# Gate projections by seven half products instead of eight, with a searched instruction order

## The chip, the cores and the metric

The kernel runs on all eight NeuronCores of one Trainium2 chip (cores 0 to 3 are one die, 4 to 7 the other). Each core computes its own share of the batch; nothing is exchanged. The metric is the device time of the slowest core in microseconds (us). In some executions, of any kernel, the cores of one or both dies show a lower granted TensorE clock and the time is longer; these are called slow (one die over 1% longer than the other at a lower clock, or the time over 1.5% above the same kernel's fastest), the others fast. Only fast executions are compared here, or, where said, the cores of an undisturbed die.

The profile's names for the engines of a core: PE is TensorE (matmuls), PEld its weight loads, DVE VectorE, ACT ScalarE, POOL GpSimd and SP SyncE. POOL and SP also issue transfers, each through its own queue; 16 DMA engines carry them. PSUM is the memory that the matmuls write to.

## The reference, cut to what matters

Four layers (D = 1024, depth 4) over 2048 prompt tokens and 64 sample tokens per core. Each layer is a chain of projections around a recurrent branch and a short convolution:

```python
h = layer_norm(x) * (1 + scale) + shift
u = h @ w_in                       # eight blocks of 1024 columns each
a_x, a_z, b_cg, b_bg, b_x, b_z, g_a, g_b = split(u)
o_a = (rglru(conv4(a_x)) * silu(a_z)) @ w_a_out
o_b = (b_bg * conv3(b_cg * b_x) * silu(b_z)) @ w_b_out
merged = sigmoid(g_a) * o_a + sigmoid(g_b) * o_b       # g_a and g_b: the two gate projections
x = layer_norm(ALPHA * x + gate * (merged @ w_o)) * ln_g + ln_b
```

The gate projections are 2 of the 11 large 1024 x 1024 products of a layer.

## The kernel before: the parts that the argument touches

The work of a core is cut into 12 slots (4 layers x 3 jobs of W = 704 tokens, HW = 352 = half a job). In each slot the first part of one job (six projections, convolutions, recurrence) is interleaved with the second part of the job before it (gates, branch outputs, output projection). The kernel writes down its operations with their dependences, and a planner in it, a list scheduler with a cost for each operation, decides the order on every engine before the program is built. The order is then fixed.

A projection of 128 output columns is 16 matmuls: 8 pieces of the contraction times 2 halves of the tokens, into one of four PSUM blocks.

```python
def mm(blk, steps, reads, tiles=(0, 1), first=True, last=True):
    def fn(e):
        for i, (w, mov) in enumerate(steps):
            for t in tiles:
                ins = e.matmul(PS[blk.pair][:, P0 + t * HW:P0 + (t + 1) * HW], w, mov(t), start=first and i == 0,
                               stop=last and i == len(steps) - 1)
        return ins
...
        for j in range(NCH):                     # 8 column groups of a slot
            def f_g(o, j=j, x=x):                # a gate: 16 matmuls, then tanh out of PSUM
                n = U.get((k, "p2", j, o))
                blk = Blk()
                mm(blk, [(wcol(WB[n], kc, 1), tile(hn, kc)) for kc in range(NCH)], [WBB[n]] + hnB)
                t = x["t" + o] = Tmp()
                act(T(t), ps(blk), AF.Tanh, [blk], [t], scale=0.5, psum=True)
            def f_o(o, j=j, x=x):                # a branch output: 16 matmuls, then gate times it
                ...
```

Weights come from HBM in fp32 and are cast to bf16 by the DMA that POOL's queue issues (`WB<-wmain`), into a ring of 8 buffers; two units for each column group.

## Time and profile before

| | before |
|---|---|
| median of 3 executions | 2721.45 us (2719.65 to 2864.68) |
| busy share of TensorE, DVE, ACT, POOL (page, slow execution) | 98%, 65%, 60%, 38% |
| matmuls per core | 18,164 |

The profile that came with the kernel fell in a slow execution of 3043 us. These are the lines of its page for the span, the busy times (engine, busy us, share, count) and the chain of work that ended last.

```profile
span 3043.2 us, 53658 instructions; the slowest of 8 cores (2984.2 to 3043.2 us)
...
PE 2972.4 (98%) x18164; PEld 1848.5 (61%) x18164; DVE 1965.9 (65%) x2316; ACT 1825.6 (60%) x2456; POOL 1158.3 (38%) x1290
...
PE 94%; DVE 2%; issue 1%; ACT 1%; DMA 1%; POOL 0%; ACTq 0%; DVEq 0%; POOLq 0%
```

TensorE is what bounds the kernel. The view of stretches of the same execution, core 0, has for each stretch the busy time and count of PE, PEld, DVE, ACT and POOL, then the granted clock, the DMA share and GB/s:

```profile
1216.00:1520.00 304.00, 303.58 (x1697) 183.40 (x1695) 199.93 (x236) 175.04 (x246) 119.21 (x143) 0.81 0.67 112
...
2432.00:2736.00 304.00, 302.62 (x2026) 198.48 (x2025) 229.41 (x259) 216.48 (x288) 132.53 (x129) 1.00 0.75 127
```

The first row runs at a clock of 0.81, the second at 1.00. At full clock a stretch of 1428 matmuls of 352 columns takes 213.5 us, 149.5 ns each. The Trainium skill, "TensorE: Matmul & The Clock Gate", Part 1, gives N/2.4 + 2.5 ns between warm matmuls, which makes an estimate of 149 ns for 352 columns, and a 13/16 limit of the clock for a die under load; both fit these numbers.

TensorE is idle for 2720.6 - 2639.4 = 81 us. By its list of waits (who waited for whom: us in total, times, longest), the largest part is the start, and nothing in the rest is large:

```profile
PE PS L971 <- DMA WB<-wc: 32.8, 7, 20.4
PE PS L479 <- ACT TMP L446: 10.3, 15, 2.7
PE PS L479 <- DVE TMP L455: 7.8, 10, 1.1
```

### The profile page before, as it was taken

The numbers are of one execution on the slowest core, as the hardware profiler recorded it, in microseconds if no ns is written. First come the engines' busy times: TensorE is split into PE (matmuls) and PEld (weight loads), VectorE is DVE, ScalarE is ACT, GpSimd is POOL, SyncE is SP. The second block draws the span as 40 slices with busy tenths as digits, with TensorE's granted clock in tenths as the row PEclk, the third lists the DMA queues.
The fourth block names the chain that finished last, engine by engine and source line by source line (L and its number), as shares of the span: only waits on it lengthen the run. The fifth ranks groups of instructions, "written<-read, shape, count | busy, mean of one in ns | idle before, by whom it ended". The sixth has DMA issues, their size and how long they took to land.

```text
span 3043.2 us, 53658 instructions; the slowest of 8 cores (2984.2 to 3043.2 us)
## 1 busy us (share of the span) xinstructions
PE 2972.4 (98%) x18164; PEld 1848.5 (61%) x18164; DVE 1965.9 (65%) x2316; ACT 1825.6 (60%) x2456; POOL 1158.3 (38%) x1290
## 2 busy tenths in 40 slices
PE   4999999999999999999999999999999999999997
PEld 2556666666666566666566666666666666666664
DVE  5666556757745664676676466458778578575674
ACT  4675547546654754655475466457667677675563
POOL 2444243334423423343442334245344345243431
PEclk8888888888888888888888888889999999999998
DMA  9669867766876786676687668777878769768774
GB/s 186 123 90 158 151 102 129 136 102 111 158 121 103 128 143 97 111 133 109 93 151 142 98 105 157 112 113 137 149 111 171 132 100 173 128 109 171 116 137 119
DMA packets 117114, 389.00 MB, mean 128 GB/s; under 512 B 13040, under 2 KB 15344, under 8 KB 116848
## 3 DMA queue, kind: packets, MB, share of 16 engines
q0 software_dynamic: 84160, 307.01, 65.3%
q1 hardware_dynamic: 32688, 78.56, 8.7%
q8 instruction: 152, 2.49, 0.3%
q14 instruction: 114, 0.93, 0.1%
HBM read 653.33 MB, written 36.27 MB: 227 GB/s over the span
## 4 chain that ended last, share of the span: by engine, by line
PE 94%; DVE 2%; issue 1%; ACT 1%; DMA 1%; POOL 0%; ACTq 0%; DVEq 0%; POOLq 0%
PE PS L479 93%; DMA WB<-wmain 1%; DVE TMP L459 1%; ACT TMP L446 1%; PE PS L971 1%; DVE TMP L455 0%; DVE LNR L455 0%; DVE TMP L697 0%; ACT L446 0%; POOL TMP L455 0%; DVE SM L455 0%; DVE X L459 0%; POOL X L485 0%; POOL WB L485 0%; DVE PS L455 0%
## 5 line engine op out<-in xcount | busy, mean ns | idle before, releaser
L479 PE MATMUL PS<-HN,WB 128*128 128x352 bf16 x12288 | 2150.3, 340 | 10.6 <-DVE TMP L455 2.7
L479 PEld LDWEIGHTS PS<-HN,WB 128*128 128x128 bf16 x12288 | 1285.1, 105 | 803.2 <-issue 15.1
L485 POOL DMA_DIRECT2D WB<-wmain x528 | 295.0, 559 | 1327.1 <-PE PS L479 1102.4
L446 ACT ACTIVATE TMP<-PS 128x704 f32<-128x704 f32 (+1 forms) x525 | 393.5, 753 | 596.0 <-PE PS L479 544.9
L446 ACT ACT_TABLE_LOAD x320 | 410.6, 1283 | 189.0 <-PE PS L479 138.5
L459 DVE SCALAR_TENSOR_TENSOR TMP<-PS,PRM,TMP 128x704 f32<-128x704 f32 (+4 forms) x467 | 430.8, 923 | 94.7 <-ACT PST L446 38.4
L455 POOL TENSOR_TENSOR TMP<-TMP 128x704 f32<-128x704 f32 (+1 forms) x225 | 392.4, 1748 | 187.9 <-ACT TMP L446 89.2
L459 DVE SCALAR_TENSOR_TENSOR TMP<-TMP,PS 128x704 f32<-128x704 f32 x192 | 170.0, 885 | 342.8 <-PE PS L479 341.4
L479 PE MATMUL PS<-MG,WB 128*128 128x352 bf16 x1536 | 273.7, 338 | 3.0 <-DVE MG L455 2.2
L479 PE MATMUL PS<-YB,WB 128*128 128x352 bf16 x1536 | 273.5, 337 | 0.0
L479 PE MATMUL PS<-YA,WB 128*128 128x352 bf16 x1536 | 273.0, 337 | 0.0
L455 DVE TENSOR_TENSOR PS<-PS,TMP 128x704 f32<-128x704 f32 x96 | 86.2, 898 | 239.4 <-ACT PS L446 133.9
L479 PEld LDWEIGHTS PS<-MG,WB 128*128 128x128 bf16 x1536 | 159.8, 105 | 101.6 <-issue 3.8
L479 PEld LDWEIGHTS PS<-YB,WB 128*128 128x128 bf16 x1536 | 159.5, 104 | 96.7
L479 PEld LDWEIGHTS PS<-YA,WB 128*128 128x128 bf16 x1536 | 159.5, 104 | 96.6
L446 ACT ACTIVATE TMP<-PS,PRM 128x704 f32<-128x704 f32 x187 | 166.3, 890 | 55.5 <-PE PS L479 38.4
L455 POOL TENSOR_TENSOR YB<-TMP 128x704 bf16<-128x704 f32 x92 | 179.1, 1947 | 53.0 <-DVE TMP L459 43.2
L446 ACT ACTIVATE TMP<-PS,HB 128x704 f32<-128x704 f32 x189 | 158.1, 845 | 66.7 <-PE PS L479 62.9
L446 ACT ACTIVATE TMP<-TMP 128x704 f32<-128x704 f32 (+1 forms) x237 | 185.1, 782 | 5.8 <-DVE MOD L459 1.4
L446 ACT ACTIVATE TMP<-X 128x704 f32<-128x704 f32 x176 | 135.0, 784 | 86.5 <-DVE X L459 66.6
L697 DVE TENSOR_TENSOR_SCAN TMP<-TMP,PST 128x704 f32<-128x704 f32 x92 | 164.4, 1787 | 30.0 <-POOL TMP L455 24.9
L455 DVE TENSOR_TENSOR TMP<-X,TMP 128x704 f32<-128x704 f32 (+1 forms) x181 | 164.8, 943 | 27.3 <-ACT TMP L446 25.1
(94 smaller groups left out, 2021.4 us busy)
## 6 DMA issues: line engine op xcount, KB each, us to landing
WB<-wmain POOLq DMA_DIRECT2D x528, 512.0 KB, 7.5
xres<-X SPq DMA_DIRECT2D x72, 352.0 KB, 12.7
X<-xres SPq DMA_DIRECT2D x72, 352.0 KB, 7.9
WB<-wc POOLq DMA_DIRECT2D x48, 512.0 KB, 7.6
X<-x SPq DMA_DIRECT2D x40, 352.0 KB, 7.7
y<-X SPq DMA_DIRECT2D x16, 352.0 KB, 13.3
X<-x POOLq DMA_DIRECT2D x8, 352.0 KB, 9.7
y<-X SPq DMA_DIRECT2D x16, 176.0 KB, 1.9
```

What stands on the lines that cost most here:

```text
L446: return P.add("act", lambda e: e.activation(out=res(out), in_=res(in_), func=func, **kw), reads, writes, cost=0.14 + 0.09 * nap + n * 0.0 ...
L455: return P.add(eng, lambda e: e.tensor_tensor(out=res(out), in0=res(in0), in1=res(in1), op=op), reads, writes, cost=cost, lat=0.05, port=n ...
L459: return P.add("dve", lambda e: e.scalar_tensor_tensor(out=res(out), in0=res(in0), scalar=scalar, in1=res(in1), op0=op0, op1=op1), reads, ...
L479: ins = e.matmul(PS[blk.pair][:, P0 + t * HW:P0 + (t + 1) * HW], w, mov(t), start=first and i == 0, stop=last and i == len(steps) - 1)
L485: return P.add(eng, lambda e: e.dma_start(out=res(out), in_=src), reads, writes, dma=tag, cost=0.56 if eng == "pool" else 0.08, nbytes=nbytes)
L697: P.add("dve", lambda e: e.tensor_tensor_scan(out=T(m)(), data0=T(r)(), data1=T(i)(), initial=PST[:, l, c, 0:1], op0=ALU.mult, op1=ALU.add ...
L971: ins = e.matmul(PS[blk.pair][:, h * 17:(h + 1) * 17], wcol(wb, kc, h), SCTb[:, kc, :], start=(kc == 0), stop=(kc == NCH - 1))
```

## The change

The intent is to take matmuls off TensorE. In 11 of the 12 slots the two gate projections of a column group are computed together by Strassen's scheme (in a form with 7 products of halves and reused sums): 7 x 4 = 28 matmuls in place of 32. For it, DVE makes four sums of the tokens per slot and four sums of the weights per column group, in bf16. The weight sums are made once per layer, stored in HBM, and read back in the other slots of the layer. Partial results hop between PSUM banks by ACT copies and DVE additions. The second part of the change is in the planner: new constants and buffer counts, and, for every group of four TensorE operations, a seed of random priorities that was found by a search (DRAWS). Core of the diff:

```diff
-NT = 18
+NT = 14
-NX = 4
-P23_FROM, P23_SPAN = 0.01, 0.85
-PE_WINDOW, EW_WINDOW = 16, 60
-QUANT = 0.25
-PE_SLACK = 1.5
+NX = 8
+P1_AT = {'ax': 0.5, 'az': 1.5, 'bz': 2.5706, 'bx': 4.207, 'gr': 4.3037, 'cg': 4.853, 'bg': 5.4886, 'gi': 6.5}
+P23_SPAN = 0.7599
+PE_WINDOW = 18
+QUANT = 0.1027
+PE_SLACK = 0.9744
  ... (more constants)
+DRAWS = (0, 0, 0, 0, 0, 0, 0, 24770, 24954, ...)      # one seed for each four TensorE operations
+            draw = DRAWS[turn] if turn < len(DRAWS) else 0
+                        if draw:
+                            key, order = key + draws[at][0], i + draws[at][1]
  ...
+    def fast_pair(k, name, hn, hnB):
+        one, two = Blk(True), Blk(True)               # two of the four PSUM blocks at once
+        c, a = one.banks
+        e, b = two.banks
+        product(a, 1, (one, two), a11, b11, [aB] + lo, True)
+        hop = act(lambda: v2(HW, W), lambda: v1(HW, W), AF.Copy, [a], [b], n=HW, psum=True)
+        product(c, 0, (), s1, t1, [bB, TSB[0]], True)
+        hop = act(T(s5, 0, HW), lambda: v1(0, HW), AF.Copy, [c], [s5], n=HW, psum=True)
+        product(b, 1, (), s2, t2, [bB, TSB[1]], False)
+        product(a, 1, (), a12, b21, [aB] + hi, False)
+        hop = tt("dve", lambda: v1(0, HW), lambda: v2(HW, W), T(s5, 0, HW), ALU.add, [b, s5], [c], n=HW, psum=True)
+        product(b, 1, (), s3, t3, [aB, TSB[2]], False)
+        hop = tt("dve", lambda: v2(0, HW), lambda: v2(HW, W), T(s5, 0, HW), ALU.add, [b, s5], [e], n=HW, psum=True)
+        product(c, 0, (), s4, b22, [bB] + hi, False)
+        product(b, 1, (), a22, t4, [aB, TSB[3]], False)
  ...
+        fast = k >= 1
+        makes = k == 1 or k > 1 and q == 0            # these slots make the weight sums and store them
+                src = (src, None) if makes else tuple(Stored(wsum_d[u, :, h * 2048:min(3584, (h + 1) * 2048)],
+                                                             wsumB[u][h], (2048, 1536)[h]) for h in range(2))
```

A gate unit read back takes two buffers of the ring of 8 (512 KB and 384 KB, on SP's queue) instead of one.

## The prediction

> What bounds it now. By the page, TensorE is busy 98% of the span; the chain of work that ended last is 94% TensorE. The profile fell in a slow execution (3043 us against a 2721 us median): the per-core list gives clocks of 0.874 to 0.895. By the stretch table core 0 ran at 0.81 up to about 2000 us and at 1.00 afterwards, core 3 the other way round. 1428 matmuls take 213.5 us at full clock (149.5 ns each), 262 take 47.3 us at 0.81 (180.6 ns). The Trainium skill, "TensorE: Matmul & The Clock Gate", Part 1, gives 352/2.4 + 2.5 = 149 ns for a warm matmul of 352 columns, and a 13/16 current limit on a die; the trace agrees with both. Joining core 3's first 1000 us (full clock) with core 0's course from the same weight load on (about 1190 us), scaled to full clock, gives about 2710 us. So the fast executions run at about full clock.
>
> At full clock 17,280 bf16 matmuls x 149.5 ns = 2583 us, the conditioning and norm matmuls about 45 us; some 85 us are start (39 us before the first large matmul, then a cold clock), tail (19 us idle in the last 83) and hardly 10 us of idle in the whole middle. No other engine is near: DVE 65%, ACT 60%, POOL 38%.
>
> What the change does. In 11 of 12 slots each of 8 column groups computes its two gate projections with 7 x 4 half matmuls instead of 32: 352 matmuls less, x 149.5 ns = 52.6 us, all on the critical engine: 1.93%.
>
> It adds, off the critical engine: 176 half-width ACT copies (352 wide out of PSUM: 0.454 us, 80 us in all), 176 half-width DVE additions on PSUM (0.52 us, 91 us), 44 token sums of 1408 bf16 and 128 weight sums of 512; scaled from the 1.02 us of a 704-wide fp32 addition these are at most 90 and 95 us, about half if bf16 goes faster. DVE so rises from 65% to at most 84%, ACT to about 70%. 56 weight loads move from POOL's queue (casting) to SP's, already in bf16; 32 units are written once. None of this should bind.
>
> The new risk is the ping-pong through PSUM: 352 times a product waits for a copy or addition of an earlier product. Counting in the built order how much TensorE work stands between (x 149.5 ns): median above 2.5 us, but 16 have 0.6 us or less and 38 under 1.0 us, against about 0.9 us for the round trip (0.45 to 0.52 us of work plus signalling). That is about 6 us of stalls if the other engines are on time, more when they are late; the tight ones gather in the last slot, where no other slot's projections fill in. The searched order can win only from start, tail and the 10 us of middle idle: I give it 5 to 12 us.
>
> 2721 - 53 + 6 - 9 = 2665 us, ratio 0.979: just at the border of 2%. Range 2648 to 2686.
>
> What would show it: 17,812 matmul records (against 18,164, give or take missing ones), still near 149.5 ns at full clock; TensorE still the chain's 90% and more; idle of TensorE before products released by ACT or DVE below 15 us in total; DVE busy up by 130 to 270 us, ACT by 80 to 110 us; start still about 39 us to the first large matmul.
>
> What would make it wrong: late hops, because ACT or DVE serves another wait first, stalling all 88 pairs by a microsecond (then 2700 or above); SP's queue holding weight loads behind stores; DVE sums slowing POOL in the scan path; the order's gain existing only in the planner; or a clock that differs between the kernels.

## More of the kernel before

Because a slow profile is a poor measure of idle time, I later ran the unchanged kernel again and got a fast profile of it (span 2720.6 us). This is what the new kernel will be compared with. Lines of its page (span, busy times, DMA queues with packets, MB and share of the engines' time, chain):

```profile
span 2720.6 us, 53658 instructions; the slowest of 8 cores (2715.0 to 2720.6 us)
...
PE 2639.4 (97%) x18164; PEld 1730.7 (64%) x18164; DVE 1974.4 (73%) x2316; ACT 1819.2 (67%) x2456; POOL 1160.6 (43%) x1290
...
q0 software_dynamic: 84160, 307.01, 69.2%
q1 hardware_dynamic: 32688, 78.56, 9.4%
...
PE 85%; DVE 6%; issue 4%; ACT 3%; DMA 2%; POOL 1%; DVEq 0%; ACTq 0%; POOLq 0%; SPq 0%
```

## The result, and the profile after

The new kernel took 2708.83 us (median of 4 fast executions, 2705.34 to 2711.49) against 2720.9 us. The ratio is 0.9955 with a 95% interval of [0.9938, 0.9973]. All ratios here are the mean time of one kernel's fast runs over that of the other's of the same rounds, so not quite the ratio of the medians. So 12 us were gained where 56 had been forecast: clear of the noise, but under 2%. The same lines of the page of its fast profile:

```profile
span 2703.8 us, 54846 instructions; the slowest of 8 cores (2676.4 to 2703.8 us)
...
PE 2594.0 (96%) x17812; PEld 1689.5 (62%) x17812; DVE 2107.1 (78%) x2664; ACT 1869.7 (69%) x2617; POOL 1120.2 (41%) x1234
...
q0 software_dynamic: 76096, 277.64, 61.8%
q1 hardware_dynamic: 58032, 159.32, 17.8%
...
PE 81%; DMA 7%; DVE 4%; issue 3%; ACT 3%; POOL 1%; DVEq 0%; ACTq 0%; SPq 0%; POOLq 0%
```

The matmuls did go: 18,164 - 17,812 = 352. TensorE's busy time fell by 2639.4 - 2594.0 = 45.4 us. But its idle time rose from 81.2 to 2703.8 - 2594.0 = 109.8 us, which gives 28.6 us back. DMA's share of the chain rose from 2% to 7%. The list of waits of the same core, core 2, shows a single wait of 12.1 us that before did not have, for stored sums, and almost nothing for the hops themselves (L597 is the line of the half products):

```profile
PE PS L1205 <- DMA WB<-wc: 33.2, 8, 20.6
PE PS L597 <- DMA WB<-wsum: 12.1, 1, 12.1
PE PS L585 <- DVE TMP L565: 10.0, 12, 2.7
PE PS L585 <- DMA WB<-wmain: 7.8, 7, 3.0
...
PE PS L597 <- DVE PS L561: 1.5, 6, 0.5
...
PE PS L597 <- ACT PS L552: 0.7, 2, 0.4
```

The view of the cores tells something else. In the new kernel, first fence, neighbouring cores end up to 26 us apart; in before (the fast profile of the repeat), second fence, 5.5 us:

```profile
core 0: 2676.4 us, clock 0.995
core 1: 2702.8 us, clock 0.992
core 2: 2703.8 us, clock 0.992
core 3: 2694.2 us, clock 0.993
```

```profile
core 0: 2715.6 us, clock 0.995
core 1: 2715.1 us, clock 0.995
core 2: 2715.0 us, clock 0.995
core 3: 2720.5 us, clock 0.993
```

Which core of a pair is the slow one changes from run to run, but in the eight fast runs of the new kernel (four here, four in a repeat below) 31 of the 32 pairs 0/1, 2/3, 4/5, 6/7 ended 9 us or more apart; in the eight fast runs of before in e1 and e17 below, none of 32 pairs did (8.9 us at most). The Trainium skill, "HBM Reference", Specifications, says that two neighbouring cores share an HBM domain and its bandwidth. The pairs agree with it; it makes memory traffic a suspect, since the new kernel writes 65.6 MB to HBM against 36.3 MB and moves 159 MB against 79 MB through the hardware queue (q1 above). In sum it is little: reads of HBM fall from 653.3 to 646.0 MB, so all of it grows by 3%. If traffic is the cause, it is more likely by when it comes than by how much there is.

The end of core 2 in the view of stretches (columns as before), and then the order of its TensorE instructions around the wait:

```profile
2605.00:2633.00 28.00, 27.56 (x183) 17.41 (x181) 17.10 (x23) 12.01 (x19) 3.17 (x6) 1.00 0.99 258
2633.00:2646.00 13.00, 0.92 (x7) 0.44 (x6) 0.89 (x1) 0.76 (x1) 0.53 (x1) 0.65 1.03 209
2646.00:2662.00 16.00, 13.65 (x73) 7.95 (x72) 5.32 (x7) 1.98 (x3) 0.00 (x0) 0.82 0.14 42
```

```profile
2633.06 0.76 PE L597 MATMUL PS<-TS,WB 128*128 128x352 bf16 x4
2645.89 2.51 PE L597 MATMUL PS<-TS,WB 128*128 128x352 bf16 x8 [12.08 <-DMA WB<-wsum]
2648.19 3.67 PE L585 MATMUL PS<-YB,WB 128*128 128x352 bf16 x16
```

For 41 us the core's DMA engines are full (share 0.99, then 1.03): in the last slot the final stores `y<-X`, the reads `X<-xres` and the stored sums all come at once. The last load of stored sums took 25.5 us from issue to landing, against a median of 5.5 us over the run; on core 0, which had come there earlier, it took 13.7 us and nobody waited. In this profile five of the eight cores have one such wait, of 11.8 to 13.4 us, and cores 0, 4 and 7 none or one of less than 6 us. It is about half of the distance between core 2 and core 0: core 2 began the same products 13 us after core 0 before it waited at all. On core 2 SP's queue waited six times, 17.5 us in all, for stores `y<-X` to land between 2600 and 2630 us, the last time just before it issued that load; on core 0, between 2586 and 2616 us, it waited for them seven times, 9.7 us. After the wait TensorE restarts at a lower clock: 16 matmuls take 3.67 us, where the same 16 take 2.55 us elsewhere in this core's trace. The skill's TensorE page, Part 1, says that an idle window of some 3.4 us halves the clock; the 0.65 and 0.82 in the clock column agree, and a narrower stretch, 2637 to 2650 us, shows 0.50 where the stretch just before (2633.9 to 2636.7) shows 1.00: the clock fell some 3 us after TensorE had gone idle.

### The profile page after: what moved, and what is told of

Read it like the earlier page. It is cut to its first block, busy times and chain, and to the rows that moved or that the text cites. A ratio compares the mean times of both kernels' runs of the same rounds, so it can differ in the third digit from the quotient of the medians.

```text
span 2703.8 us, 54846 instructions; the slowest of 8 cores (2676.4 to 2703.8 us)
## 1 busy us (share of the span) xinstructions
PE 2594.0 (96%) x17812; PEld 1689.5 (62%) x17812; DVE 2107.1 (78%) x2664; ACT 1869.7 (69%) x2617; POOL 1120.2 (41%) x1234
## 3 DMA queue, kind: packets, MB, share of 16 engines
q0 software_dynamic: 76096, 277.64, 61.8%
q1 hardware_dynamic: 58032, 159.32, 17.8%
HBM read 645.99 MB, written 65.63 MB: 263 GB/s over the span
## 4 chain that ended last, share of the span: by engine, by line
PE 81%; DMA 7%; DVE 4%; issue 3%; ACT 3%; POOL 1%; DVEq 0%; ACTq 0%; SPq 0%; POOLq 0%
PE PS L585 70%; PE PS L597 11%; DVE TMP L565 2%; DMA WB<-wc 2%; DMA WB<-wmain 2%; ACT TMP L552 2%; DMA X<-x 1%; DMA WB<-wsum 1%; DMA wsum<-WB 1%; DVE TMP L561 1%; PE PS L1205 1%; DVE MG L561 0%; ACT L552 0%; DVE PS L561 0%; DMA y<-X 0%
## 5 line engine op out<-in xcount | busy, mean ns | idle before, releaser
L585 PE MATMUL PS<-HN,WB 128*128 128x352 bf16 x9472 | 1483.5, 313 | 30.3 <-DVE TMP L565 8.2
L585 PEld LDWEIGHTS PS<-HN,WB 128*128 128x128 bf16 x9472 | 922.7, 98 | 527.4 <-issue 42.9
L603 POOL DMA_DIRECT2D WB<-wmain x472 | 263.4, 559 | 909.9 <-PE PS L585 464.1
L552 ACT ACTIVATE TMP<-PS 128x704 f32<-128x704 f32 (+1 forms) x603 | 418.8, 709 | 294.8 <-PE PS L585 134.4
L561 DVE TENSOR_TENSOR PS<-PS,TMP 128x352 f32<-128x352 f32 (+1 forms) x267 | 173.1, 652 | 131.8 <-PE PS L597 62.3
L597 PE MATMUL PS<-TS,WB 128*128 128x352 bf16 x1408 | 260.8, 313 | 15.2 <-DMA WB<-wsum 12.1
L585 PE MATMUL PS<-YB,WB 128*128 128x352 bf16 x1536 | 247.3, 315 | 6.1 <-POOL YB L561 2.6
L585 PE MATMUL PS<-YA,WB 128*128 128x352 bf16 x1536 | 244.6, 312 | 1.2 <-DVE WB L690 0.7
L585 PE MATMUL PS<-MG,WB 128*128 128x352 bf16 x1536 | 240.9, 314 | 3.1 <-DVE MG L561 2.3
L585 PEld LDWEIGHTS PS<-YB,WB 128*128 128x128 bf16 x1536 | 150.4, 99 | 88.3 <-issue 8.4
L585 PEld LDWEIGHTS PS<-MG,WB 128*128 128x128 bf16 x1536 | 149.8, 98 | 84.0 <-issue 4.6
L585 PEld LDWEIGHTS PS<-YA,WB 128*128 128x128 bf16 x1536 | 149.4, 98 | 81.5 <-issue 3.8
L597 PE MATMUL PS<-HN,WB 128*128 128x352 bf16 x1056 | 199.3, 312 | 0.3 <-DVE PS L561 0.3
L597 PEld LDWEIGHTS PS<-TS,WB 128*128 128x128 bf16 x1408 | 134.9, 98 | 92.6 <-issue 22.4
```

The source lines that it names most:

```text
L552: return P.add("act", lambda e: e.activation(out=res(out), in_=res(in_), func=func, **kw), reads, writes, cost=0.14 + 0.09 * nap + n * 0.0 ...
L561: return P.add(eng, lambda e: e.tensor_tensor(out=res(out), in0=res(in0), in1=res(in1), op=op), reads, writes, cost=cost, lat=0.05, port=n ...
L597: ins = e.matmul(ps(blk)(half * HW, (half + 1) * HW), w(i), mov(i), start=first and i == 0, stop=i == 3, skip_group_check=True)
L603: return P.add(eng, lambda e: e.dma_start(out=res(out), in_=src), reads, writes, dma=tag, cost=0.56 if eng == "pool" else 0.08, nbytes=nbytes)
```

## The experiments

Two theories stood at the start. Theory 1: the hops between half products, and what they hold, stall TensorE. Theory 2: the memory traffic of the stored sums does. A third, added later: the sums make DVE late. Labels give the order of the runs.

### 1. Before, again

No edit.

> The kernel before, unchanged, for a profile in the fast state. Theory 1 (the new kernel loses its matmul saving in idle time of TensorE): span about 2717 us on the slowest core, idle of TensorE in the middle (152 us to the last slot) under 15 us, so that the new kernel's 41 us there is new. Rival (the before kernel has the same idle at full clock and its matmuls are simply slower per piece): 30 us or more of middle idle here too. Also looked at: whether of each pair of neighbouring cores one ends 25 us later, as in the new kernel (2676 against 2703); theory 2 (memory traffic of the stored sums) expects a spread under 10 us here.

It ran 2722.44 us, and is the fast profile shown above. Adding up the idle gaps before TensorE's matmuls from 152 us to 120 us before the end gives 18 us on its slowest core; the new kernel's slowest core has 38. That is a little above theory 1's 15 us and far below the rival's 30, so about half of the middle idle is new, and the spread between neighbours (at most 5.5 us here) is new as well.

### 2 to 4. The parts of the change apart

```diff
# e2_no_draws
-            draw = DRAWS[turn] if turn < len(DRAWS) else 0
+            draw = 0
# e3_plain_no_draws: the same, and
-        fast = k >= 1
+        fast = False
# e4_last_plain (with the seeds)
-        fast = k >= 1
+        fast = 1 <= k < NSLOT - 1
```

> The new kernel with all seeded priorities set to 0, everything else as it is; the planner's own estimate goes from 2647 to 2714 us. Theory (the search is what hides the hops between half products, and the chip keeps about half of what the plan promises): 2735 to 2760 us, 1 to 2% slower than the new kernel. Rival (the search fits the planner's model only, the chip sees none of it): within 10 us of the new kernel, 2700 to 2718 us.

> The new kernel with whole gate products in every slot (no half products, no sums, no stored sums) and priorities 0; what stays of the change is its planner constants, buffer counts and unit layout. The planner estimates 2701 us against 2710 for before. Theory (without half products a plan is kept on the chip within 10 us): 2705 to 2715 us, that is as fast as the whole change. Rival (planner constants are worth nothing on the chip): 2718 to 2725 us.

> The new kernel with whole gate products in the last slot alone: 32 matmuls (4.8 us) more, 16 loads of stored sums less, and priorities that no longer fit in the last 80 us (planner: 2661 against 2647 us). Theory (the slowest core loses 12 us to a late load of stored sums at the end and some 4 us to the cold clock after it): the slowest core loses no time to stored sums at the end; 2695 to 2705 us in spite of the worse plan. Rival (the end is not what makes the core slow, it only falls there): 2715 to 2725 us, as the plan says.

Fast runs of the same job, before at a mean of 2722.3 us:

| kernel | half products | searched seeds | planner's own estimate, us | chip, us (fast runs) |
|---|---|---|---|---|
| before | no | no | 2710 | 2722.3 |
| e3_plain_no_draws | no | no | 2701 | 2705.9 (2704.93 to 2706.82) |
| e2_no_draws | yes | no | 2714 | 2742.2 (2740.63, 2743.77) |
| the new kernel | yes | yes | 2647 | 2708.6 (first job) |
| e4_last_plain | not in the last slot | yes | 2661 | 2705.7 (2705.25 to 2706.58) |

For e3 one more run counts as fast (2732.22 us); there two cores of one die ran at a clock of 0.983 and took 2730 us while the others took 2698 to 2710. I leave it out of the mean; with it the ratio is 0.997 [0.990, 1.004].

The planner's part of the change alone, with whole products, gains 16 us and reaches the time of the whole change. (That part is the constants, some rules of the planner, the buffer counts and the layout of the weight units, not separated here. Contrary to what was expected, e3 still makes the 44 token sums, which nothing reads: 2360 DVE instructions against before's 2316.) Half products without the search then cost 36 us, although they take 352 matmuls away; the search takes 34 us off again. The ranges of the theories held for e3 (2705 to 2715 us) and for e2 (2735 to 2760). The pages of e2 and e3, the lines of the span and of busy times, in this order:

```profile
span 2742.2 us, 55056 instructions; the slowest of 8 cores (2725.6 to 2742.2 us)
...
PE 2607.8 (95%) x17812; PEld 1683.6 (61%) x17812; DVE 2160.8 (79%) x2664; ACT 1901.1 (69%) x2639; POOL 1137.0 (41%) x1234
```

```profile
span 2704.3 us, 53956 instructions; the slowest of 8 cores (2697.5 to 2704.3 us)
...
PE 2630.6 (97%) x18164; PEld 1728.9 (64%) x18164; DVE 2030.1 (75%) x2360; ACT 1821.0 (67%) x2457; POOL 1149.5 (43%) x1290
```

Idle time of TensorE is 2742.2 - 2607.8 = 134.4 us with half products and 73.7 us without. Busy time falls by only 22.8 us, not by 52.6: the modelled end of a matmul (313 ns after its start, while the next can start after 149.5) hides about 0.16 us of every wait, and a clock that drops after a longer wait makes matmuls longer. The mean granted clocks, 0.995 and 0.997, leave at most some 6 us to the clock. Where the idle time stands is shown by the groups of TensorE instructions (busy us, mean ns, then idle time before them and its releasers), e2 first, e3 second:

```profile
L585 PE MATMUL PS<-HN,WB 128*128 128x352 bf16 x9472 | 1491.2, 313 | 38.5 <-ACT TMP L552 16.0 <-DMA WB<-wmain 9.8 <-DVE TMP L565 6.1
L597 PE MATMUL PS<-TS,WB 128*128 128x352 bf16 x1408 | 262.5, 313 | 17.7 <-DVE PS L561 12.3 <-ACT PS L552 2.3 <-DVE MOD L565 0.8
```

```profile
L585 PE MATMUL PS<-HN,WB 128*128 128x352 bf16 x12288 | 1907.2, 313 | 19.9 <-ACT TMP L552 6.9 <-DMA WB<-wmain 4.1 <-DVE SM L561 2.5
```

Only 12.3 + 2.3 us of it stand at the half products themselves, waiting for a hop. The whole products (L585), which are 2816 fewer here, wait 38.5 us instead of 19.9, for ACT, which frees PSUM, and for weights. A half-product pair holds two of the four PSUM blocks from its first product to its last, and its sums take two of the eight weight buffers. That this is what makes the others wait fits the lines, but no run here changed the number of blocks or buffers, so it is argued and not shown.

In e4 the wait for stored sums at the end is gone, and yet the time is only 3 us better. Its planned order is 14 us worse than the new kernel's (2661 against 2647): 4.8 us are the 32 matmuls more, the rest probably seeds that no longer fit. The expectation (2695 to 2705 us) was missed by less than 1 us; the run does not say how much the end costs. That needed the same order.

### 5 to 8. Same order, one cost made tiny

In these four kernels the order of every instruction on TensorE, DVE, ACT and POOL is that of the new kernel (compared on the built programs); only sizes change. Their outputs are wrong, which doesn't matter for the times. Three of the four still passed the comparison with the reference (e7 failed, with a relative error of 0.021); that says nothing of their correctness.

```diff
# e5_tiny_stored: stored sums 64 columns wide, in both directions
-                    load("sp", WB[s][:, 0:src.n], src.ap, [src.buf], ...
+                    load("sp", WB[s][:, 0:64], src.ap[:, 0:64], [src.buf], ...
-        load("sp", wsum_d[u, :, 0:2048], wa[:, :], ...
+        load("sp", wsum_d[u, :, 0:64], wa[:, 0:64], ...
-        load("sp", wsum_d[u, :, 2048:3584], wb[:, 0:1536], ...
+        load("sp", wsum_d[u, :, 2048:2112], wb[:, 0:64], ...
# e6_tiny_hops: each of the four hops of a pair 8 columns wide, for example
-        hop = act(lambda: v2(HW, W), lambda: v1(HW, W), AF.Copy, ...
+        hop = act(lambda: v2(HW, HW + 8), lambda: v1(HW, HW + 8), AF.Copy, ...
# e7_tiny_sums: weight sums, and token sums after the first slot, 8 columns wide
-            P.add("dve", lambda e: e.tensor_tensor(out=out, in0=in0, in1=in1, op=op), ...
+            P.add("dve", lambda e: e.tensor_tensor(out=out[:, 0:1, 0:8], in0=in0[:, 0:1, 0:8], in1=in1[:, 0:1, 0:8], op=op), ...
# e8_tiny_all: all three
```

> The new kernel, same instructions in the same order on TensorE, DVE, ACT and POOL, but the stored sums are written and read back only 64 columns wide instead of 2048 and 1536 (wrong result on purpose). Theory 2 (memory traffic of the stored sums: the late load at the end, and the 25 us between neighbouring cores): every core at 2670 to 2685 us, neighbours within 8 us, time about 2682 us. Rival theory 1 (the hops between half products are what stalls TensorE, the loads only come late because of it): 2700 us or more, neighbours still 20 us or more apart.

> The new kernel, same instructions in the same order, but the 352 copies and additions between half products work on 8 columns instead of 352 (wrong result on purpose; about 0.37 us less each, 65 us of ACT and 65 us of DVE). Theory 1 (hops): 2680 us or less on the slowest core, the middle idle of TensorE down from 41 us to under 20. Theory 2 (stored sums): slowest core 2695 us or more, neighbours still 20 us or more apart.

> The new kernel, same instructions in the same order, but the weight sums and the token sums work on 8 columns (wrong result on purpose; some 100 us of DVE less). Theory 3 (the sums make DVE late for TensorE, DVE being 78% busy): 2690 us or less. Theories 1 and 2: within 6 us of 2708 us.

> All three together, same order (wrong result on purpose). If hops, sums and stored sums are all that keeps the new kernel from its gain, it runs near the planner's estimate of 2647 us plus the 10 us that before runs above its own: 2650 to 2662 us. If something else is missing (the order itself, other waits that the half products make): 2670 us or more.

| kernel | fast runs, mean us | against the new kernel's 2708.5 (its 8 fast runs) | ratio to before |
|---|---|---|---|
| e5_tiny_stored | 2683.7 | -25 | 0.9858 [0.9815, 0.9900] |
| e6_tiny_hops | 2703.8 | -5 | 0.9933 [0.9904, 0.9962] |
| e7_tiny_sums | 2702.2 | -6 | 0.9926 [0.9897, 0.9955] |
| e8_tiny_all | 2671.7 | -37 | 0.9814 [0.9772, 0.9856] |

The traffic of the stored sums is the largest single cost in the new kernel's order: 25 us. Theory 2 is borne out in the main by the cores too. In the profile of e5 neighbours are 9 to 12 us apart, not 26; that is more than the 8 us expected, so a part of the spread has another cause, which is open (view of the cores):

```profile
core 0: 2682.6 us, clock 0.994
core 1: 2670.3 us, clock 0.996
core 2: 2681.4 us, clock 0.995
core 3: 2672.5 us, clock 0.995
```

Theory 1 falls as far as the length of the hops goes: shrinking all 352 gives 5 us, and theory 3 gives 6. (What a pair holds between its products, the other half of theory 1, was not changed by any run.) Both are small: the new kernel's own runs differ by up to 6 us (2705.34 to 2711.49), and the intervals of e6 and e7 overlap its 0.9955 [0.9938, 0.9973]. Together the three give 37 us, about their sum. Still, 2671.7 us is 10 us more than the 2650 to 2662 that would have meant that nothing else is missing. The page of e8:

```profile
span 2671.2 us, 54846 instructions; the slowest of 8 cores (2659.7 to 2671.2 us)
...
PE 2584.2 (97%) x17812; PEld 1689.4 (63%) x17812; DVE 2001.4 (75%) x2664; ACT 1822.6 (68%) x2617; POOL 1118.1 (42%) x1234
```

It still idles 87 us, more than the 73.7 us of e3 which has whole products and no search. What remains is in waits that a tiny cost does not remove; which ones is open.

### 9 to 12, and 13 to 18. Which traffic, and the search without half products

I wrote a search of my own for the planner's seeds: for each group of four TensorE operations it tries 24 to 40 seeds, plans on for 12 to 16 groups, and keeps the seed with the least idle time. The planner was told that ACT operations take 0.02 us longer (as calibrated on the trace: a planned 0.735 us took 0.754) and that loads land later. Whole products with such an order is plain_search; half products except in the last slot is half_search. The other two kernels are again in the new kernel's order:

```diff
# tiny_loads: only the reads of the stored sums are 64 columns wide
-                    load("sp", WB[s][:, 0:src.n], src.ap, ...
+                    load("sp", WB[s][:, 0:64], src.ap[:, 0:64], ...
# tiny_last_loads: only those of the last slot
+                    m = src.n if self.seq[n][0][0] < NSLOT - 1 else 64
+                    load("sp", WB[s][:, 0:m], src.ap[:, 0:m], ...
# plain_search: fast = False; half_search: fast = 1 <= k < NSLOT - 1; both:
-cost=0.14 + 0.09 * nap
+cost=0.16 + 0.09 * nap
-                op.finish = dma_free + 1.2
+                op.finish = dma_free + 3.0          # half_search: 1.8
+DRAWS = (seeds of the new search)
```

The first call fell on a chip on which no execution of before was undisturbed (2829 us and more, clocks down to 0.86), so its four kernels tell nothing:

> Whole gate products in every slot, the new kernel's planner constants, and priorities from a search of my own (24 to 32 draws for each group of four TensorE operations, kept by the idle time 16 groups on; the planner told of a DMA latency 1.8 us longer and ACT operations 0.02 us longer). Planner: 2690 us, against 2701 without search. Theory (the search is worth as much without half products; half products buy nothing here): 2690 to 2700 us, faster than the new kernel's 2708. Rival (half products are needed for the gain): 2705 us or more.

> The new kernel, same order; the stored sums are written in full but read back only 64 columns wide (wrong result on purpose). Tells apart which direction of the stored sums' traffic costs the 25 us that tiny_stored showed. If the reads do it: 2680 to 2688 us. If the 64 writes (about 10 us each to landing, holding a weight buffer meanwhile) do it: 2698 us or more.

> The new kernel, same order; only the 16 loads of stored sums of the last slot are 64 columns wide (wrong result on purpose). Theory (the one late load of the last slot and the cold clock after it are the largest part of the 25 us): 2688 to 2696 us, slower neighbours still 9 us or more behind. Rival (the traffic costs its time all along): 2702 us or more.

> Half products in slots 2 to 11, whole products in the last, and the same kind of own search (40 draws, DMA latency 0.6 us longer than the new kernel's planner has it). Planner: 2683 us. If the chip adds what it added to the new kernel outside the last slot (25 us): 2700 to 2710 us. If a planner that knows longer latencies gives orders that hold: 2688 to 2698 us, as good as or better than the searched whole products.

They were taken again in two calls, the second with the new kernel itself beside them:

> As e9, taken again because no run of e9 was fast: whole gate products with a searched order; planner 2690 us. Theory (the half products buy nothing here that an order of whole products doesn't): 2690 to 2700 us. Rival: 2705 us or more.

> As e12, taken again for the same reason: half products in slots 2 to 11 with a searched order; planner 2683 us. If the chip adds what it added to the new kernel outside the last slot (25 us): 2700 to 2710 us, slower than e13. If orders planned with longer latencies hold: 2688 to 2698 us.

> As e10, taken again. If the reads of the stored sums cost the time: as tiny_stored, slowest core 2680 to 2688 us (on an undisturbed die). If the 64 writes do: 2698 us or more.

> As e11, taken again. If the late load of the last slot and the cold clock after it are the largest part: slowest core of an undisturbed die 2686 to 2696 us, neighbours still 9 us or more apart. If the traffic costs its time all along: 2702 us or more.

> The new kernel unchanged, on the chip of the other three: 2703 to 2711 us on an undisturbed die, slowest core.

> Whole products with a searched order beside the new kernel: slowest core of an undisturbed die 2696 to 2701 us, 5 to 12 us less than e17, if half products buy nothing that a searched order of whole products doesn't; equal or more than e17 if they do.

In the first of these calls the second die ran at clocks of 0.982 to 0.991 in the fast runs of every kernel, so I compare the undisturbed die, cores 0 to 3, in fast runs: plain_search 2697.7, 2697.1 and 2699.2 us (slowest of the four cores), half_search 2717.6, 2723.9, 2722.0 and 2723.8 us, before 2718.5 to 2724.2 us. The ratios of whole times are 0.9912 [0.9877, 0.9948] and 0.9951 [0.9931, 0.9970], with the throttled die in them. So plain_search kept its expectation on this die, and half_search missed both of its outcomes (2700 to 2710 and 2688 to 2698): it is as slow as before.

In the second call all dies were undisturbed in the fast runs:

| kernel | fast runs, mean us | ratio to before |
|---|---|---|
| e17_after_again, the new kernel | 2708.3 | 0.9955 [0.9932, 0.9979] |
| e15_tiny_loads_2 | 2691.7 | 0.9896 [0.9867, 0.9925] |
| e16_tiny_last_loads_2 | 2693.1 | 0.9900 [0.9876, 0.9924] |
| e18_plain_search_3 | 2701.3 | 0.9930 [0.9906, 0.9953] |

Reads of stored sums cost 17 of the 25 us, and the 16 of the last slot alone 15: the expectation of e16 held (2686 to 2696 us, and its neighbours still end 11 to 16 us apart in the profile). The result of e15 lies between its two outcomes: reads do the most of it, and by difference about 8 us are left for the 64 writes (e5 and e15 stand in different calls and their intervals overlap, so this is not clear of noise). So what looked like a cost all along falls mostly in the last slot. That it is there the one late load of the traces, and the clock that falls after it, fits, but all 16 reads were made small at once.

And whole products with a searched order beat both kernels: 2701.3 us, 7 us less than the new kernel and 19 less than before's 2720.4 in the same call. Its neighbours are within 6 us of each other. Its products are those of before; like e3 it also makes 44 token sums that nothing reads (2360 DVE instructions). Its page:

```profile
span 2700.0 us, 53879 instructions; the slowest of 8 cores (2694.1 to 2700.0 us)
...
PE 2633.8 (98%) x18164; PEld 1729.4 (64%) x18164; DVE 2023.7 (75%) x2360; ACT 1814.5 (67%) x2447; POOL 1155.6 (43%) x1290
```

66 us of idle are left, of which 38 stand in the first 152 us. One pattern runs through all of it: with whole products the chip takes 5 to 12 us more than the planner's estimate (before 2710 and 2722, e3 2701 and 2706, plain_search 2690 and 2701). With half products it takes 28 us more unsearched (2714 and 2742), 61 us more in the new kernel (2647 and 2708), 45 more without them in the last slot (e4, 2661 and 2706), and about 40 more with my search (2683 and some 2722 on the undisturbed die). Part of the new kernel's 61 us is shown above to be traffic: the planner has one DMA rate and a fixed latency, and does not know of a 25 us landing.

## Why the prediction was wrong, point by point

- "What bounds it", TensorE at about full clock: right. The fast profile of before has 2639.4 us of TensorE work in 2720.6 us.
- "352 matmuls less, x 149.5 ns = 52.6 us": the count was exact. Busy time fell by 45.4 us; the rest was not traced further.
- "None of this should bind": this is the step that failed. It said that the added work runs beside TensorE and costs nothing. Narrowing it showed 25 us for the stored sums' traffic and 6 us for the sums on DVE, in an order whose search also had to hide them. That is at most 31 of the 44 us between the forecast 2665 and the measured 2709; the rest is not accounted for one by one, and e8, with the hops made tiny as well, is still 7 us above the forecast. Unsearched, half products lost 36 us where 53 were to be saved: some 89 us, 61 of them more idle time of TensorE, in place of the 6 us of stalls in my sum. Why whole products wait longer there, blocks and buffers held, is argued and not shown.
- "About 6 us of stalls" at the hops: right in size for the new order (2.2 us of direct waits, 1.5 + 0.7 in the lines shown; 5 us when narrowed), but it was the wrong place to look. I counted the distances between a product and the one that needs its hop, and not what a pair holds and moves meanwhile.
- "I give it 5 to 12 us" for the order: undersized. The planner's part without seeds is worth 16 us with whole products, the seeds 34 us with half products and, in a search of my own with an altered planner, 3 to 5 us more with whole products (3 when each kernel is set against before of its own call). The two large errors had opposite signs: -16 + 36 - 34 = -14 us, close to the measured -12, where I had -53 + 6 - 9 = -56. That the forecast missed by 44 us and not by the 83 of the half products (+36 for -47) is luck: the search, undersized by 41, made good half of it.
- "SP's queue holding weight loads behind stores" was named among the things that could go wrong. What happened is near it: a load of stored sums took 25.5 us, and SP's queue had waited for a store just before it issued it. Saturated DMA engines in the last slot are shown; whether the queue's order or the neighbour's traffic decides is not separated.
- Idle of TensorE before products released by ACT or DVE below 15 us: right for the half products (2.2 us). Taken over all products it is wrong: the two lists of waits add to 39 us in the new kernel and to 32 already in before.
- DVE up by 130 to 270 us: right, 2107.1 - 1974.4 = 133, but partly by luck. The added parts take 92.7 (hops), 70.5 (weight sums) and 40.3 us (token sums), 203.5 in all; DVE's other instructions, as many as before, became 71 us shorter, and why was not looked into. The token sums took 0.88 to 0.95 us for 1408 bf16 elements, half of what fp32 would take by my scaling.
- ACT up by 80 to 110 us: wrong, 51. The half-width copies cost 82 us as costed (42.3 and 39.5 us), but 15 table loads fewer saved 19 us, and other work shrank a little.
- TensorE at 90% of the chain or more: wrong, 81%. In a fast execution it is 85% even before.
- Start at 39 us: right, 39.6 us against 39.7.

## What to carry to other kernels

When a change has two parts, run each alone before crediting either: here the planner's part with the old products gave the whole gain, and half products with their search gave nothing on top. Work saved on the bounding engine must be set against everything the saving holds and moves (accumulator blocks, buffers, traffic in the busiest stretch), not only against the direct wait that it makes. A plan that promises much more than its predecessor is a claim to be checked against a trace, mechanism by mechanism, since a search can lean on whatever the model does not know.

## What the Trainium skill lacked or had wrong

- "TensorE: Matmul & The Clock Gate", Part 1, says that dense matmuls on three or more cores of a die bring the clock to 13/16 within 5 to 20 us and keep it there, and advises to budget 1.95 GHz for all cores. Here all eight cores ran dense matmuls for 2.7 ms at a mean granted clock of 0.99 or more in the executions whose dies were undisturbed; 0.81 came only in some executions of the same program, or in parts of one. The page exempts one or two busy cores and operands of all zeros or all ones; neither holds here (the reference draws its inputs from a normal distribution).
- The same page, "Back-to-back issue gap", gives about 131 ns per matmul for a stream of weight loads and matmuls of 512 columns, and calls N/2.4 + 2.5 an overcount for large N. The stream here, a weight load with every matmul of 352 columns, ran at 149.5 ns each, as the formula has it.
- "HBM Reference" says that neighbouring cores share bandwidth, about 358 GB/s each. It lacks what that means for a kernel well below this: at 263 GB/s of HBM reads and writes on average (the page's own line; 163 GB/s counted at the DMA queues), one core of a pair ended 9 us or more after the other in 31 of 32 pairs, and the lot changed between runs. The traffic of the stored sums makes most of this distance (e5); that the shared bandwidth is how it does so is not shown.
- "DMA: Bandwidth & Descriptors" says that casting loads must go through POOL's queue. No page that I read says what they cost: here the casting queue took 61.8% of the engines' time for 277.64 MB, the other 17.8% for 159.32 MB: 4.5 MB against 9.0 MB for each per cent. If the queue's count is of bf16, as the page's HBM line suggests (645.99 MB read, of which twice 277.64 is 555), both move 9.0 MB per per cent, and a casting load costs the engines what its fp32 source weighs.
